# Hymba and PEER layer on one core: every fourth expert row of the first token half added on VectorE, and the steps around the gathers re-cut

## Chip, cores and metric

The kernel runs on one core of a Trainium2 chip. The metric is device time in microseconds of one execution. Before: 876.36 us, the median of three runs (872.04 to 880.57). What can be told from no change with such runs is about 1%.

## What is computed

The reference takes 256 tokens of width 1024 (float32) through one layer:

```python
h = rms_norm(x, attn_norm)
mq, mk, mv, dq, dk, dv = split(h @ w_in)          # six groups of 512 columns
a_out = moba_attention(rope(norm(mq)), rope(norm(mk)), mv)      # 8 heads x 64, causal
b_out = diff_attention(rope(norm(dq)), rope(norm(dk)), dv, lam) # 4 heads, softmax1 - lam*softmax2
x = x + concat(norm(a_out), norm(b_out)) @ w_out
# PEER, of xc = rms_norm(x):
q = (xc @ w_query).reshape(C, 8, 2, 128)
sc = einsum('thpd,hpnd->thpn', q, sub_keys)        # 8 heads x 2 x 128 scores
experts, gates = top 16 of the 16 x 16 sums of the two top 16's, softmax
u, vv = expert_down[experts], expert_up[experts]   # 128 rows of each per token
w = gates * gelu(einsum('cd,chkd->chk', xc, u))
x = x + einsum('chk,chkd->cd', w, vv)
```

With 256 positions there is one MoBA block, so group A is plain causal attention. Most of the data is the last part: 256 tokens x 128 experts x 8 KB of rows, 268 MB.

## The kernel before

The tokens form two halves of 128, A and B, with a token on each partition. The two expert tables lie side by side in DRAM, so that one indirect DMA (`in_uv_dram`, line 598) brings for one expert slot the down row and the up row of each of 128 tokens: 128 rows of 8 KB, 1.049 MB. There are 256 such **slots**, 0 to 127 for half A and 128 to 255 for half B. One slot is worked off so:

- `issue` (POOL, L598) starts the gather into a free buffer of a ring, if the slot's index is known (`ready`);
- `dot` (DVE, L608) multiplies the down row with the normalised token and sums: the slot's scalar `hdot`;
- `weigh` (ACT, L614, L615, L617) takes gelu, multiplies with the gate, and scales an identity matrix by the result: `dg`;
- `add` (PE, L627) multiplies `dg` with the up row, two products of 512 columns (each in float32 two passes, so x4 in the trace), summed in PSUM over the 128 slots of a half; then the buffer is free and `issue` is called.

`slots(1)` writes `dot` of slot n, `weigh` and, one slot behind, `add` of slot n-1. The buffers come in three pools: 4 (`gat0`) from the start, 5 more (`gat1`) once the projections of half B are through and their tiles freed, 6 more (`gat2`) once half B has left attention.

Ahead of the gathers run attention and output projection of half A, then `query`, `keys`, `route1` and `route2` for the first two PEER heads: product with the query weights, scores against the keys, the top 16 of each half by MAX8, FIND_INDEX8 and MATCH_REPLACE8 on DVE, candidate sums on POOL and DVE, index matching (`hit`, L550 on DVE and L553 on POOL) and the list `eid` of expert indices. This gives 32 ready slots. Up to there a scheduler orders the instructions. From `manual_schedule` on (end of the function) they stand as they are written: the generator `behind` yields all that is left of half A's routings and of half B (projections, attention, output projection, four routings) in small steps, and the main loop takes a fixed number of steps for each slot:

```python
while done[0] < NT * NSEL:
    slots(1)
    while steps < STEPS * (done[0] + 1):
        next(work, None)
        steps += 1
    issue()
```

Each engine works its queue strictly in order, so a step that waits holds up the slot work that is written behind it on the same engine. Weights come by DMAs from the SP queue (L88), 0.524 MB each, four for a group: `w_in` through a ring of eight tiles (`wts`), `peer_query` through four, `w_out` of half A through `wts` as well and of half B through four tiles that are there once attention is done (`wo2`).

Of the kernel before, what the change touches and what calls it, by code (L numbers as in the profile page):

```python
# [20 lines left out]
P = 128  # L21
# [27 lines left out]
STEPS = 1.45  # L49
# [3 lines left out]
def hymba_peer_kernel(ctx, tc, xT_d, x_d, an_d, fn_d, fnT_d, win_d, qkg_d, lam_d, og_d, wout_d,  # L53
# [9 lines left out]
    psA = ctx.enter_context(tc.tile_pool(name="psA", bufs=4, space=PSUM))  # L63
    psB = ctx.enter_context(tc.tile_pool(name="psB", bufs=2, space=PSUM))
# [3 lines left out]
    gat0 = ctx.enter_context(tc.tile_pool(name="gat0", bufs=RING0))  # L68
# [109 lines left out]
    def proj(ci, tt):  # L178
        p = pps[ci, tt] = psB.tile([P, 512], FT, name="psB")
        for k in range(KC):  # L180
            PE.matmul(p, lhsT=xT[tt][:, k], rhs=W[ci + 6 * tt][k // 2][:, k % 2], start=(k == 0), stop=(k == KC - 1))  # L181
            if k % 2:
                yield
# [215 lines left out]
    for g in (3, 0, 1):  # L399
        fetch(g, win_d[g], wts)  # L400
# [4 lines left out]
    for g in (5, 4):  # L405
        fetch(g, win_d[g], wts)
# [25 lines left out]
    for q in range(4):  # L432
        for n in range(2):
            fetch(("o", n, A), wout_d[n], wts, (q,))
# [31 lines left out]
    def query(tt, c4):  # L466
        w = W["q", c4]
        q = rt1.tile([P, 4, P], FT, name="qs", tag="qs")
        p = ps().rearrange("p (a b) -> p a b", b=P)
        for c in range(4):  # L470
            for k in range(KC):
                PE.matmul(p[:, c], lhsT=w[k // 2][:, k % 2, c * P:(c + 1) * P], rhs=xgT[tt][:, k],  # L472
                          start=(k == 0), stop=(k == KC - 1))
            if c < 3:
# [3 lines left out]
        yield

    def keys(tt, c4):  # L480
        sc = scp.tile([P, 4, NKEY], FT, name="sc")
        p = ps().rearrange("p (a b) -> p a b", b=NKEY)
        q = qs.pop((tt, c4))
        for c in range(4):
            PE.matmul(p[:, c], lhsT=q[:, c], rhs=sk[:, c4 * 4 + c], start=True, stop=True)  # L485
        S.activation(sc.rearrange("p a b -> p (a b)"), p.rearrange("p a b -> p (a b)"), AF.Copy, scale=r2[tt])  # L486
        scs[tt, c4] = sc
# [12 lines left out]
    def route1(tt, c4):  # L500
        sc = scs.pop((tt, c4))
        ts_ = rt1.tile([P, 2, 2, TOPK], FT, name="tops", tag="tops")
        ti = rt1.tile([P, 2, 2, TOPK], U32, name="topi", tag="topi")
        s2 = rt1.tile([P, 4, NKEY], FT, name="s2", tag="s2")
        hm = [(ts_[:, n // 2, n % 2], ti[:, n // 2, n % 2], sc[:, n], s2[:, n]) for n in range(4)]
# [24 lines left out]
        best = rt1.tile([P, 2, TOPK], FT, name="best", tag="best")  # L530
        pos = rt1.tile([P, 2, TOPK], U32, name="pos", tag="pos")
        s3 = rt1.tile([P, 2, NCAND], FT, name="s3", tag="s3")
        for h in range(2):
# [252 lines left out]
```

## Time and profile before

| | |
|---|---|
| runs | 876.36 us (872.04 to 880.57) |
| the profiled execution | 878.93 us, of which 877.2 us are the span from the first to the last instruction |
| granted TensorE clock, mean | 0.965 of full speed |
| busy in the span | PE 725.2, DVE 497.9, POOL 401.1, ACT 311.8 us |
| DMA | 323.16 MB, mean 368 GB/s; 268.85 MB of it by the gathers' queue |

Busy time of PE is modelled and long; the chain of waits and the tables of busy time by stretch say more. A DMA's time from issue to data is seen only in what waits for it.

### The profile page before, as it was taken

What the parts mean: (1) busy time and instruction counts of PE and PEld (TensorE: products, weight loads), DVE (VectorE), ACT (ScalarE), POOL (GpSimd) and SP (SyncE); (2) the same over time, 40 slices, a digit from 0 to 9 for tenths busy, and PEclk for the clock granted to TensorE, in tenths of its full rate; (3) what the DMA queues carried; (4) which work ended last, traced back from release to release, by engine and by line L of the source; (5) the groups of instructions that cost most, each with busy time, mean ns of one, the idle gap of its engine ahead of it and who ended that gap; (6) DMA issues with size and microseconds to landing.
All of it is one profiled execution on the core that took longest, in us unless ns stands there. A gap on an engine that the chain in (4) does not pass through costs nothing.

```text
span 877.2 us, 8338 instructions
## 1 busy us (share of the span) xinstructions
PE 725.2 (83%) x2156; PEld 337.4 (38%) x2156; DVE 497.9 (57%) x1364; ACT 311.8 (36%) x936; POOL 401.1 (46%) x426
## 2 busy tenths in 40 slices
PE   6998858597599888877989889799777787787776
PEld 2554543253245445433635545243222222222222
DVE  4753663764663776750577575874444454455443
ACT  1322112333242573621343352443333333333332
POOL 3310333562542573311654656675555555555540
PEclk9999969999999899988999999999999999999999
DMA  9969559989997999996999999999999999999993
GB/s 352 350 200 363 204 194 381 382 295 390 418 343 263 396 386 421 349 344 241 344 417 417 418 418 419 420 420 420 421 419 420 421 418 420 421 420 421 420 419 153
DMA packets 52687, 323.16 MB, mean 368 GB/s; under 512 B 6240, under 2 KB 6496, under 8 KB 19744
## 3 DMA queue, kind: packets, MB, share of 16 engines
q0 software_dynamic: 36944, 268.85, 76.0%
q1 hardware_dynamic: 15264, 53.12, 16.3%
q10 hardware_dynamic: 432, 0.66, 0.2%
q8 instruction: 18, 0.29, 0.1%
q14 instruction: 29, 0.24, 0.1%
HBM read 321.55 MB, written 1.05 MB: 368 GB/s over the span
## 4 chain that ended last, share of the span: by engine, by line
DMA 47%; PE 33%; DVE 9%; issue 5%; ACT 3%; POOL 2%; SPq 0%; DVEq 0%; POOLq 0%; ACTq 0%
DMA uv<-in_uv_dram,eid 43%; PE acc L627 14%; PE psB L181 7%; PE psA L472 4%; DVE uv L608 3%; DMA w<-in_wout_dram 3%; PE psB L350 3%; PE psA L252 1%; POOL hit L553 1%; PE psA L301 1%; POOL uv L598 1%; DMA w<-in_win_dram 1%; PE psA L485 1%; PE psA L251 1%; ACT dg L617 1%
## 5 line engine op out<-in xcount | busy, mean ns | idle before, releaser
L627 PE MATMUL acc<-uv,dg 128*128 128x512 f32 x1024 | 505.4, 625 | 110.3 <-ACT dg L617 107.6
L598 POOL DMA_INDIRECT uv<-in_uv_dram,eid x256 | 319.7, 1249 | 362.9 <-PE acc L627 182.6
L608 DVE SCALAR_TENSOR_TENSOR uv<-uv,xn 128x1024 f32<-128x1024 f32 x256 | 315.5, 1243 | 220.6 <-DMA uv<-in_uv_dram,eid 210.5
L627 PEld LDWEIGHTS acc<-uv,dg 128*128 128x128 f32 x1024 | 183.1, 194 | 395.5 <-ACT dg L617 235.5
L614 ACT ACTIVATE hdot<-hdot 128x1 f32<-128x1 f32 x256 | 51.3, 200 | 332.1 <-DVE uv L608 312.6
L617 ACT ACTIVATE dg<-ident,hdot 128x128 f32<-128x128 f32 x256 | 102.8, 402 | 48.5 <-PE acc L627 40.8
L181 PE MATMUL psB<-w,xT 128*128 128x512 f32 x192 | 90.8, 615 | 7.2 <-DMA w<-in_win_dram 7.2
L615 ACT ACTIVATE hdot<-hdot,gate 128x1 f32<-128x1 f32 x256 | 75.3, 294 | 8.3
L472 PEld LDWEIGHTS psA<-xgT,w 128*128 128x128 f32 x512 | 63.2, 198 | 11.7 <-issue 11.6
L472 PE MATMUL psA<-xgT,w 128*128 128x128 f32 x512 | 63.1, 280 | 0.0
L181 PEld LDWEIGHTS psB<-w,xT 128*128 128x128 f32 x192 | 36.5, 197 | 49.1 <-issue 46.6
L495 POOL TENSOR_TENSOR ci<-tf 128x4 f32<-128x4 f32 (+3 forms) x72 | 22.6, 344 | 56.8 <-DVE tf L523 56.7
L350 PE MATMUL psB<-w,mT 128*128 128x512 f32 x64 | 32.3, 640 | 8.3 <-DMA w<-in_wout_dram 7.6
L507 DVE MAX8 tops<-sc 128x8 f32<-128x128 f32 x32 | 7.0, 281 | 36.9 <-ACT sc L486 30.6
L567 DVE TENSOR_REDUCE ef<-hit 128x16 f32<-128x320 f32 (+1 forms) x16 | 11.5, 732 | 26.6 <-POOL hit L553 26.6
L553 POOL TENSOR_TENSOR hit<-hit,ci 128x160 f32<-128x160 f32 (+1 forms) x32 | 25.8, 838 | 0.9 <-DVE hit L550 0.7
L212 POOL TENSOR_TENSOR qt<-pr,rS 128x128 f32<-128x128 f32 (+1 forms) x24 | 14.1, 613 | 19.4 <-ACT pr L193 19.3
L358 DVE TENSOR_TENSOR x<-psB,x 128x512 f32<-128x512 f32 x4 | 2.8, 691 | 33.9 <-PE psB L350 33.9
L350 PEld LDWEIGHTS psB<-w,mT 128*128 128x128 f32 x64 | 12.4, 202 | 23.7 <-issue 12.8
L608 DVE DVE_READ_ACCUMULATOR uv<-uv,xn 128x1 f32 x256 | 21.4, 83 | 0.0
L476 ACT COPY qs<-psA 128x512 f32<-128x512 f32 x8 | 4.7, 582 | 33.2 <-PE psA L472 33.2
L226 PE MATMUL psA<-ident,qo 128*128 128x128 f32 x32 | 5.8, 311 | 12.4 <-DVE qo L219 12.4
(125 smaller groups left out, 410.3 us busy)
## 6 DMA issues: line engine op xcount, KB each, us to landing
w<-in_win_dram SPq DMA_DIRECT2D x48, 512.0 KB
w<-in_wq_dram SPq DMA_DIRECT2D x28, 512.0 KB
w<-in_wout_dram SPq DMA_DIRECT2D x16, 512.0 KB
uv<-in_uv_dram,eid POOLq DMA_INDIRECT x256
sk<-in_sk_dram SPq DMA_DIRECT2D x1, 1024.0 KB
out_dram<-x SPq DMA_DIRECT2D x4, 256.0 KB
xT<-in_xT_dram SPq DMA_DIRECT2D x2, 256.0 KB
x<-in_x_dram ACTq DMA_DIRECT2D x1, 512.0 KB
```

The source lines that it names most:

```text
L181: PE.matmul(p, lhsT=xT[tt][:, k], rhs=W[ci + 6 * tt][k // 2][:, k % 2], start=(k == 0), stop=(k == KC - 1))
L212: G.tensor_tensor(tv[:, :, m, a], prv[:, :, m, b], ropeS[tt][:, None, g0 + m, a].to_broadcast([P, nh, 32]), op=OP.mult)
L350: PE.matmul(wops[tt, n], lhsT=mixT[tt, MOBA if k < 4 else DIFF][:, k % 4], rhs=W["o", n, tt][k // 2][:, k % 2], start=(k == 0), stop=(k == ...
L472: PE.matmul(p[:, c], lhsT=w[k // 2][:, k % 2, c * P:(c + 1) * P], rhs=xgT[tt][:, k], start=(k == 0), stop=(k == KC - 1))
L495: eng.tensor_tensor(d, src[:, :, 1, b0:b0 + nb], src[:, :, 0, a0:a0 + 1].to_broadcast([P, 2, nb]), op=OP.add)
L553: G.tensor_tensor(e[:, h], e[:, h], ci[:, h, None, :n].to_broadcast([P, 8, n]), op=OP.mult)
L598: G.indirect_dma_start(out=rows[n], out_offset=None, in_=uv_d, in_offset=bass.IndirectOffsetOnAxis(ap=eid[tt][:, k:k + 1], axis=0))
L608: V.scalar_tensor_tensor(uv[:, :D], uv[:, :D], 1.0, xn[n // NSEL], op0=OP.mult, op1=OP.mult, accum_out=h)
L614: S.activation(h, h, AF.Gelu)
L615: S.activation(h, h, AF.Copy, scale=gate[n // NSEL][:, col:col + 1])
L617: S.activation(dg, ident, AF.Copy, scale=h)
L627: PE.matmul(acc[tt][:, c], lhsT=dg, rhs=uv[:, D + c * 512:D + (c + 1) * 512], start=(k == 0), stop=(k == NSEL - 1))
```

## The change

Five edits, which the diff shows together:

- **DVE adds.** For slots n of half A with n % 4 == 1 (32 slots) `weigh` stops after the gate, and `add` is one DVE instruction over 128x1024 that adds the up row times the slot's scalar to `x2[A]` in SBUF. The two products and `dg` are left out for these slots.
- **Finer steps.** A projection yields after each product of 512 columns (before: after two), a query after each four of 128, the output projection after each; STEPS goes from 1.45 to 2.0. One step is taken ahead of the first slot.
- **First routing by head.** The query of heads 0 and 1 is computed ahead, but scores and routing of head 0 alone; this gives 16 ready slots. Head 1 is the first work among the slots. The functions of the routing take the head and the number of heads.
- **Value weights kept.** Groups 5 and 4 (the values) of `w_in` stay in `wts` for half B, which projects 5, 4 and 2 ahead of the gathers (before: 2 and 3) and 3, 0, 1 among the slots (before: 0, 1, 5, 4). `w_out` of half A has eight tiles of its own, in room that `gat0` takes over.
- **Pools.** psA has 3 tiles for 4, psB 3 for 2, `hdot` 8 for 6.

```diff
-STEPS = 1.45
+STEPS = 2.0
+
+DVE_ADD = 4
...
-    psA = ctx.enter_context(tc.tile_pool(name="psA", bufs=4, space=PSUM))
-    psB = ctx.enter_context(tc.tile_pool(name="psB", bufs=2, space=PSUM))
+    psA = ctx.enter_context(tc.tile_pool(name="psA", bufs=3, space=PSUM))
+    psB = ctx.enter_context(tc.tile_pool(name="psB", bufs=3, space=PSUM))
...
-    gat0 = ctx.enter_context(tc.tile_pool(name="gat0", bufs=RING0))
+    wos = ExitStack()
+    wo1 = wos.enter_context(tc.tile_pool(name="wo1", bufs=8))
...
-            if k % 2:
-                yield
+            yield
...
-            fetch(("o", n, A), wout_d[n], wts, (q,))
+            fetch(("o", n, A), wout_d[n], wo1, (q,))
...
+    wos.close()
...
+        for a, b in parts:
+            p = ps().rearrange("p (a b) -> p a b", b=P)
+            for c in range(a, b):
+                for k in range(KC):
+                    PE.matmul(p[:, c], lhsT=w[k // 2][:, k % 2, c * P:(c + 1) * P], rhs=xgT[tt][:, k],
+                              start=(k == 0), stop=(k == KC - 1))
+                    if k % 4 == 3 and (c, k) != (b - 1, KC - 1):
+                        yield
+            S.copy(q[:, a:b], p[:, a:b])
+            yield
...
+    def choose(tt, c4, h0=0, nh=2):
+        yield from keys(tt, c4, 2 * h0, 2 * h0 + 2 * nh)
+        yield from route1(tt, c4, h0, nh)
+        yield
+        route2(tt, c4, h0, nh)
+        ready[0] += nh * TOPK
...
         S.activation(h, h, AF.Copy, scale=gate[n // NSEL][:, col:col + 1])
+        if n < NSEL and n % DVE_ADD == 1:
+            ready_w.append((n, h))
+            return
...
-        for c in range(2):
+        if n < NSEL and n % DVE_ADD == 1:
+            V.scalar_tensor_tensor(x2[tt], uv[:, D:], dg, x2[tt], op0=OP.mult, op1=OP.add)
+        for c in range(0 if n < NSEL and n % DVE_ADD == 1 else 2):
...
-    run(route(A, 0, 1))
+    run(query(A, 0, ((0, 2), (2, 4))))
+    load_q(1, wqp)
+    run(choose(A, 0, 0, 1))
...
-        fetch(g + 6, win_d[g], wts)
+        if g < 4:
+            fetch((g, B), win_d[g], wts)
+        else:
+            W[g, B] = W[g, A]
...
-    run(project(2), project(3))
+    run(project(5), project(4), project(2))
+    gat0 = ctx.enter_context(tc.tile_pool(name="gat0", bufs=RING0))
     rings += [gat0] * RING0
...
-        for g in (0, 1, 5, 4):
+        for g in (3, 0, 1):
             yield from project(g)
...
                     wout(B, n, k, psB)
-                yield
+                    yield
...
+        yield from choose(A, 0, 1, 1)
         yield from mix(route(A, 1, 2), f, 2, 1)
...
     work = behind()
+    for _ in range(1):
+        next(work)
```

POOL's queue before, around the first gathers; `ci` are candidate sums, `hit` index matches, `qt` and `qo` the rope of half B's projections, `uv<-in_uv_dram` a gather:

```order
L553 TENSOR_TENSOR hit_796<-hit_796,ci 128x160 x2
L553 TENSOR_TENSOR hit_800<-hit_800,ci 128x400 x2
L217 TENSOR_TENSOR qo<-qo,qt 128x512
L598 DMA uv<-in_uv_dram,eid_671 128x2048
L212 TENSOR_TENSOR qt<-pr,rS_833 128x8x32 x2
L598 DMA uv<-in_uv_dram,eid_671 128x2048
L217 TENSOR_TENSOR qo<-qo,qt 128x512
L598 DMA uv<-in_uv_dram,eid_671 128x2048 x11
```

The same place in POOL's queue after the change:

```order
L556 TENSOR_TENSOR hit_782<-hit_782,ci 128x160
L556 TENSOR_TENSOR hit_785<-hit_785,ci 128x400
L604 DMA uv<-in_uv_dram,eid_672 128x2048 x4
L214 TENSOR_TENSOR qt<-pr,rS_817 128x8x32 x2
L219 TENSOR_TENSOR qo<-qo,qt 128x512
L604 DMA uv<-in_uv_dram,eid_672 128x2048
L498 TENSOR_TENSOR ci<-tf 128x8
```

The matches ahead of the first gather are two instead of four, and four gathers stand ahead of the rope, which before stood between them.

DVE's queue before, from the first `dot` (`uv,hdot<-uv,xn`) on; `MAX`, `MAX_INDEX` and `MATCH_REPLACE` belong to the routing of heads 2 and 3:

```order
L608 SCALAR_TENSOR_TENSOR uv,hdot<-uv,xn_652 128x1024
L219 TENSOR_TENSOR qo<-qo,rsq 128x512
L608 SCALAR_TENSOR_TENSOR uv,hdot<-uv,xn_652 128x1024 x3
L507 MAX tops<-sc 128x8 x4
L608 SCALAR_TENSOR_TENSOR uv,hdot<-uv,xn_652 128x1024 x2
L510 MAX_INDEX topi<-tops,sc 128x8 x4
L513 MATCH_REPLACE s_1055<-tops,sc 128x128 x4
L608 SCALAR_TENSOR_TENSOR uv,hdot<-uv,xn_652 128x1024 x2
```

DVE's queue after the change at slots 5 to 12 (`x_105<-uv,hdot,x_105` is the new add; the first row is the `dot` of slots 5 and 6):

```order
L614 SCALAR_TENSOR_TENSOR uv,hdot<-uv,xn_653 128x1024 x2
L636 SCALAR_TENSOR_TENSOR x_105<-uv,hdot,x_105 128x1024
L614 SCALAR_TENSOR_TENSOR uv,hdot<-uv,xn_653 128x1024 x4
L636 SCALAR_TENSOR_TENSOR x_105<-uv,hdot,x_105 128x1024
L614 SCALAR_TENSOR_TENSOR uv,hdot<-uv,xn_653 128x1024
L510 MAX tops<-sc 128x8 x4
L614 SCALAR_TENSOR_TENSOR uv,hdot<-uv,xn_653 128x1024
```

An add of slot n stands behind the `dot` of slot n+1, so it also waits for that slot's rows. By the order of PE's queue, the scores of half B's attention begin at slot 44 before and at slot 54 after, and its residual stands at slot 80 to 82 in both.

## Rows read from the trace of the kernel before

**Rows 1.** Busy time of each engine by stretch, the span in seven parts
```profile
core 0: us, PE busy (x) PEld busy (x) DVE busy (x) ACT busy (x) POOL busy (x), PEclk, DMA share, GB/s
0.00:111.00 111.00, 97.63 (x348) 51.51 (x348) 62.91 (x237) 27.57 (x69) 26.94 (x45) 0.98 0.79 290
111.00:152.00 41.00, 30.21 (x123) 18.54 (x124) 18.95 (x56) 9.70 (x26) 13.46 (x13) 0.85 0.78 292
152.00:279.00 127.00, 101.50 (x326) 49.65 (x325) 74.71 (x220) 41.93 (x120) 60.02 (x77) 0.97 0.92 354
279.00:421.00 142.00, 120.13 (x370) 58.67 (x370) 80.21 (x210) 62.94 (x179) 53.72 (x60) 0.92 0.91 347
421.00:581.00 160.00, 141.13 (x514) 76.87 (x513) 117.97 (x410) 64.81 (x190) 100.38 (x125) 0.96 1.01 414
581.00:868.00 287.00, 230.65 (x473) 80.81 (x471) 140.65 (x228) 103.89 (x349) 146.59 (x108) 1.00 0.99 411
```

**Rows 2.** One source line in a stretch, L608: 152:279, 279:421, 421:581, 581:868
```profile
L608 DVE SCALAR_TENSOR_TENSOR uv<-uv,xn x36: 1210/1226/2679, 152.1 to 274.8; 128x1024 f32<-128x1024 f32 x36
L608 DVE SCALAR_TENSOR_TENSOR uv<-uv,xn x39: 1211/1222/3548, 279.2 to 417.5; 128x1024 f32<-128x1024 f32 x39
L608 DVE SCALAR_TENSOR_TENSOR uv<-uv,xn x59: 1206/1222/1324, 421.4 to 578.6; 128x1024 f32<-128x1024 f32 x59
L608 DVE SCALAR_TENSOR_TENSOR uv<-uv,xn x114: 1224/1226/1227, 581.1 to 865.8; 128x1024 f32<-128x1024 f32 x114
```

**Rows 3.** The chain that ended last, by line, 581:877, 279:421 and 152:279
```profile
by line: DMA uv<-in_uv_dram,eid 91.6%; issue 3.4%; PE acc L627 2.6%; DVE uv L608 0.4%; DVE x L634 0.2%; DVEq L782 0.2%; POOLq L598 0.2%; ACT dg L617 0.1%; ACT hdot L615 0.1%; POOLq L782 0.1%; ACT hdot L614 0.1%; DVEq L608 0.0%
by line: PE acc L627 40.8%; DMA w<-in_wout_dram 16.9%; PE psB L350 10.0%; PE psA L252 4.8%; PE psA L301 3.8%; issue 2.9%; PE psA L249 2.6%; ACT L614 1.8%; PE psA L251 1.8%; PE psA L289 1.5%; PE psB L181 1.2%; ACT ex L263 1.1%; ACT L558 0.9%
by line: DMA uv<-in_uv_dram,eid 42.6%; PE acc L627 17.0%; PE psB L181 9.5%; issue 8.9%; DVE uv L608 7.9%; PE psA L472 5.5%; POOL uv L598 3.1%; POOL hit L553 2.6%; ACT dg L617 1.0%; DVE cs L495 0.5%; ACT hdot L615 0.5%; ACT hdot L614 0.3%; D
```

**Rows 4.** Timeline of DVE and POOL, first routing to first gather
```profile
95.86 0.87 DVE L507 MAX8 tops<-sc 128x8 f32<-128x128 f32 x4 [5.59 <-ACT sc L486]
...
105.50 3.93 POOL L553 TENSOR_TENSOR hit<-hit,ci 128x160 f32<-128x160 f32 x4 [0.74 <-DVE hit L550]
109.39 1.26 POOL L217 TENSOR_TENSOR qo<-qo,qt 128x512 f32<-128x512 f32 x1
111.14 1.03 POOL L598 DMA_INDIRECT uv<-in_uv_dram,eid  x1 [0.49 <-DVE rs_a L123]
```

**Rows 5.** Timeline of DVE and POOL, first slots
```profile
118.66 1.22 DVE L608 SCALAR_TENSOR_TENSOR uv<-uv,xn 128x1024 f32<-128x1024 f32 x1
...
126.04 1.22 DVE L608 SCALAR_TENSOR_TENSOR uv<-uv,xn 128x1024 f32<-128x1024 f32 x1 [2.44 <-DMA uv<-in_uv_dram,eid]
...
129.91 0.94 POOL L598 DMA_INDIRECT uv<-in_uv_dram,eid  x1 [10.92 <-PE acc L627]
...
140.01 0.87 DVE L507 MAX8 tops<-sc 128x8 f32<-128x128 f32 x4 [12.73 <-ACT sc L486]
...
152.09 1.23 DVE L608 SCALAR_TENSOR_TENSOR uv<-uv,xn 128x1024 f32<-128x1024 f32 x1 [2.53 <-DMA uv<-in_uv_dram,eid]
```

**Rows 6.** Groups by line in 152:279: busy us, mean ns | idle before
```profile
L627 PE MATMUL acc<-uv,dg 128*128 128x512 f32 x138 | 69.5, 629 | 25.5 <-ACT dg L617 25.5
L608 DVE SCALAR_TENSOR_TENSOR uv<-uv,xn 128x1024 f32<-128x1024 f32 x36 | 46.4, 1288 | 49.3 <-DMA uv<-in_uv_dram,eid 44.2 <-ACT hdot L614 2.4 <-ACT qk L228 1.6
```

**Rows 7.** The chain in order of time, 279:425, pieces
```profile
305.61 9.87 PE acc L627 x16
...
369.51 15.34 DMA w<-in_wout_dram
384.89 4.12 PE psB L350 x6
389.01 2.14 PE acc L627 x4
391.15 1.72 PE psB L350 x4
392.87 1.72 PE acc L627 x4
394.58 0.87 PE psB L350 x2
...
395.47 8.71 DMA w<-in_wout_dram
```

**Rows 8.** One source line, L88 (loads of weights), from 111 us on
```profile
L88 SPq DMA_DIRECT2D w<-in_wq_dram x20: 328/368/547, 131.9 to 499.5; - x20
L88 SPq DMA_DIRECT2D w<-in_win_dram x12: 328/632/990, 133.9 to 211.8; - x12
L88 SPq DMA_DIRECT2D w<-in_wout_dram x8: 327/328/538, 368.7 to 396.3; - x8
```

**Rows 9.** Nearest row to the new add, and gather issues in 279:421 and 581:840
```profile
L376 DVE SCALAR_TENSOR_TENSOR xn<-x,r,fn x2: 1283/1284/1286, 88.7 to 426.4; 128x1024 f32<-128x1024 f32 x2
L598 POOL DMA_INDIRECT uv<-in_uv_dram,eid x44: 932/937/1966, 281.2 to 420.6; - x44
L598 POOL DMA_INDIRECT uv<-in_uv_dram,eid x104: 937/1371/1723, 581.0 to 838.1; - x104
```

More of the change, by code (lines that the diff above doesn't have):

```diff
@@ L399, in hymba_peer_kernel @@
     for g in (3, 0, 1):
[L400 removed]
+        fetch((g, A), win_d[g], wts)
     bcast(og, og_d, D)
@@ L464, in load_q, with query, keys @@
         fetch(("q", c4), wq_d[c4], pool)
-    def query(tt, c4):
+    def query(tt, c4, parts=((0, 4),)):
         w = W["q", c4]
         q = rt1.tile([P, 4, P], FT, name="qs", tag="qs")
[L469 to L474, printed above, removed]
-                yield
-        S.copy(q, p)
-        qs[tt, c4] = q
[L478 to L487, printed above, removed]
+        qs[tt, c4] = q
+        for a, b in parts:
[8 more added lines that the diff above has]
+            yield
+    def keys(tt, c4, a, b):
+        sc = scp.tile([P, 4, NKEY], FT, name="sc")[:, :b - a]
+        p = ps().rearrange("p (a b) -> p a b", b=NKEY)[:, :b - a]
+        for c in range(a, b):
+            PE.matmul(p[:, c - a], lhsT=qs[tt, c4][:, c], rhs=sk[:, c4 * 4 + c], start=True, stop=True)
+        S.activation(sc, p, AF.Copy, scale=r2[tt])
+        scs[tt, c4, a] = sc
         yield
@@ L529, in route1 @@
         yield
[L530 to L533, printed above, removed]
+        best = rt1.tile([P, 2, TOPK], FT, name="best", tag="best")[:, :nh]
+        pos = rt1.tile([P, 2, TOPK], U32, name="pos", tag="pos")[:, :nh]
+        s3 = rt1.tile([P, 2, NCAND], FT, name="s3", tag="s3")[:, :nh]
+        for h in range(nh):
             V.max(best[:, h, :8], cs[:, h])
-        for h in range(2):
+        for h in range(nh):
             V.max_index(pos[:, h, :8], best[:, h, :8], cs[:, h])
-        for h in range(2):
+        for h in range(nh):
             V.match_replace(s3[:, h], best[:, h, :8], cs[:, h], -3.0e38)
         yield
-        for h in range(2):
+        for h in range(nh):
             V.max(best[:, h, 8:], s3[:, h])
-        for h in range(2):
+        for h in range(nh):
             V.max_index(pos[:, h, 8:], best[:, h, 8:], s3[:, h])
-        posf = rt1.tile([P, 2, TOPK], FT, name="posf", tag="posf")
+        posf = rt1.tile([P, 2, TOPK], FT, name="posf", tag="posf")[:, :nh]
         V.tensor_copy(posf, pos)
@@ L713, in behind @@
         yield from mix(route(A, 3), f, 1, 1)
-        yield from f
+        for _ in f:
+            yield
         yield from route(B, 3, 2)
```

66 lines of the change are left out of this document (30 added, 36 removed).

## Prediction

> **What bounds the kernel now.** I read the busy table by stretch first, then the chain of waits, then single lines in the stretches where the chain changes its nature.
>
> From 421 us on the DMA engines move 411 to 414 GB/s [rows 1]. From 581 us the chain is 91.6% the gathers' own DMA [rows 3], and VectorE's `dot` comes at an even pace: 114 of them between 581.1 and 865.8, so 2.52 us a slot [rows 2]. Nothing that an engine does there can shorten the end; only fewer bytes or an earlier start of this steady stream can. Ahead of it the DMA moves 290, 292, 354 and 347 GB/s [rows 1]. Measured against 414 GB/s, the stretches from 111 to 421 us waste 41 x 0.29 + 127 x 0.14 + 142 x 0.16 = 53 us. That is what a change of the order can win.
>
> Who wastes it differs. Around 111 to 152 us the chain is broken up by queue order: the fifth gather waits 10.9 us for PE to free a buffer, and `dot` of slot 4 stands behind a MAX8 that waits 12.7 us for its scores [rows 5]. From 152 to 279 us, with four buffers, the chain is 42.6% gather, with PE pieces adding up to some 32% [rows 3]; VectorE waits 44.2 us for landings, and 36 slots take 127 us, 3.53 each [rows 2, 6]. From 279 to 421 us, attention and output projection of half B, the chain is PE's: 40.8% slot products, and 16.9% the wait for `w_out` [rows 3].
>
> So I forecast by landmarks: the first gather, slot 7, slot 54 (where attention begins after the change), slot 82, and the end. Before, these are: first issue 111.1, slot 7 at 152.1, slot 82 at 421.4 [rows 2, 4, 5]. From slot 82 both kernels have the same DMA work left, so the remaining 455.8 us are carried over.
>
> **The change part by part.**
>
> *First gather.* From the first MAX8 to the first issue 15.3 us pass [rows 4]. One head halves every round: five rounds over 128 columns like the one of 0.87 save at least 5 x 0.43 = 2.2; two instead of four matches on POOL save 3.93 / 2 = 2.0; half B's rope (1.26 on POOL) and its twin on DVE leave the queues ahead of the issue, together with halved match instructions some 2.3, an estimate from these rows. Sum 6.5 us: first issue at 104.6. Bounds: 4.2 (only the two sure items) to 8.
>
> *First slots.* The first gather's `dot` came 7.5 us after its issue [rows 4, 5]. DVE then has eight dots (1.31 with the read of the sum: 10.5), two adds (2.6), and routing and projection work, which before was 18.95 - 7 x 1.31 = 9.8 us in this stretch [rows 1, 2]; about as much, as half a routing and one projection stand there now. In sum 7.5 + 10.5 + 2.6 + 9.8 = 30.4; I add 2 us of waits: slot 7 at 137, 15 earlier than before. What allows it is that PE's first slot product now stands right behind the projections and the two turns are gone from in front of it. If half of the 12.7 us wait comes back, it is 143; the lower bound is 133.
>
> *Four-buffer stretch, slots 7 to 53.* 47 gathers at 2.52 are 118.4 us. Loads beside them: two query groups and two projection groups, 16 x 1.26 (half a gather's bytes each) = 20.2 us. The DMA floor is thus 138.6, or 2.95 a slot. PE's slot product falls from 69.5 / 36 = 1.93 a slot [rows 6] to three quarters, 1.45. DVE gets dearer: the nearest row to the add is a scale-and-multiply over 128x1024 with a scalar from SBUF, 1.28 us [rows 9]; `dot` itself took 1.23 and at worst 3.55 [rows 2]; I take 1.28, with 1.2 and 3.55 as ends. Before, DVE was busy 74.71 us in 36 slots, 2.08 each [rows 1]; other work than dots was 25.3. Now 47 x 1.31 + 12 x 1.28 + some 36 (one more routing) = 113, or 2.40 a slot. All three are below 3.53; the best is 2.95, and I take 3.2: 150 us, slot 54 at 287. Ends: 138.6 (DMA alone) and 47 x 3.53 = 166 (the pace of before).
>
> *Attention stretch, slots 54 to 81.* Before, 38 slots stood here, now 28, of which 21 have a PE product. The chain's slot products were 0.408 x 142 = 57.9 us; 21/38 of it is 32.0, a gain of 25.9. Seven adds of 1.28 are 9.0 on DVE; DVE is on this chain only in part, so I charge half, 4.5. PSUM pool psA with three tiles makes the second pair of score tiles wait for the first exponentials; no row shows it, between 0 and 8 us (two groups, about one `ex` and `mx` round each); I take 2. The waits for `w_out`, 15.3 and 8.7 us [rows 7], stay: its four tiles still come when attention ends. 142 - 25.9 + 6.5 = 122, slot 82 at 409. Ends: 110 (with fewer products PE also waits less for `dg`) and 142.
>
> *Value weights.* Eight loads, 4.2 MB, 10 us of DMA, are gone. But before the change 12 loads of `w_in` and 20 of the query weights follow the first gather [rows 8]; after it groups 3, 0 and 1 and the same queries do. The saved loads fall into the first 111 us, at 290 GB/s [rows 1], where PE and DVE set the pace: worth nothing. The same holds for the earlier `w_out` of half A.
>
> *Finer steps, STEPS 2.0.* They move work, cost no instruction, and their effect is in the slot numbers above.
>
> *Behind slot 82.* DVE has 117.97 of 160 us [rows 1]; eleven adds bring 14 more: 132. The DMA stays the limit.
>
> Sum: 137 + 150 + 122 = 409, against 421.4: 12 us less. The profiled execution took 878.93 us, so 866.9; it lies 0.3% above the median of the runs, and on their scale I predict 864 us.
>
> **The rivals.**
>
> *DMA alone sets the pace.* PE relieved, everything runs at the floor: 137 + 138.6 + 110 = 386, 36 less, 841 us. For it: between 581 and 868 us the stream needs no more than this. Against it: fifteen buffers there, four here.
>
> *Attention keeps its 142 us.* The steps come two to a slot, so that dependent steps (scores, maximum, exponential) meet without slot work between, and PE idles where it used to multiply. 137 + 150 + 142 = 429, 8 more: 884 us. For it: the chain hops to ACT and DVE in this stretch already. Against it: 40.8% of it is products of which many are gone.
>
> *The adds block POOL.* A gather's issue takes 0.937 us at the median in the attention stretch and 1.371 where dots run regularly beside it [rows 9]: one engine waits for the other. Fourteen adds fall into the time of four buffers, where each issue is urgent. At 0.43 each this is 6 us, at a whole add of 1.28 each 18: 137 + 150 + 122 + 18 = 427, 882 us. The Trainium skill (SBUF — State Buffer, section SBUF: two separate sides) says that a VectorE instruction with two SBUF inputs and a GpSimd instruction share a port pair that one of them holds for its whole length, the other being blocked. By that rule the add is such an instruction; the trace agrees for `dot`, with the two medians above.
>
> *Slower: VectorE becomes the bound with four buffers.* An add sits in order behind the next `dot`, so DVE's waits for landings cannot be filled. If they stay as long as before, 44.2 / 36 = 1.23 a slot [rows 6], and the 0.22 of other waits too, a slot takes 2.40 + 1.23 + 0.22 = 3.85, the stretch 181 us, and slot 82 comes at 440: 19 more, 895 us. It decides from 3.45 us a slot on; there the change only breaks even. Against it: waits for landings normally shrink when DVE comes later to them.
>
> **How the numbers follow.** A measurement of this kernel tells about 1% from no change. The forecast has 0.50, of which 0.44 lies over 1% below; DMA alone 0.14; attention unchanged 0.14 and the blocked POOL 0.08, both within 1%; VectorE-bound 0.14, of which 0.12 is over 1% slower. So faster 0.58, same 0.30, slower 0.12. The range goes from the DMA's case, 841, to just past the unchanged attention, 886; the likeliest case alone spans 850 to 876.
>
> **What would show it.** Right: first gather near 105 us, slot 7 near 137, the scores of half B's attention near 287, slot 82's `dot` near 409, an even 2.5 us from slot 141, and no wait for a matched index or a score above 5 us among the first slots. The slot products' share of the chain in attention should fall to about a quarter. Wrong: 3.5 us a slot or more with four buffers while DVE is over 85% busy (VectorE-bound); attention over 135 us with PE waiting for ACT or DVE; issues of 1.5 us and more beside the adds; or the DMA below 400 GB/s between slots 90 and 140, which would mean that the added DVE work limits there too.

## The result, and the profile after

885.6 us at the median of 11 runs (882.63 to 894.72), against 877.05 (872.04 to 881.01) for the kernel before in the same series: 1.0107 times as long, 95% interval 1.0074 to 1.0140. The forecast was 864 and faster, inside a range of 841 to 886; the change is slower by 1%. The profiled execution took 884.77 us, its span is 883.0 (before 877.2).

The landmarks are starts of `dot`, in us from the span's start. The forecast has slot 82 as its landmark; slot 84 stands here too, since the last step of half B's layer (projection, residual, norm) stands there in both kernels, and the last six buffers open.

| | before | forecast | after | after minus before, step by step |
|---|---|---|---|---|
| slot 0 | 118.7 | 112.1 | 112.8 | -5.9 |
| slot 7 | 152.1 | 137 | 138.4 | -7.8 |
| slot 54 | 313.2 | 287 | 309.8 | +10.3 |
| slot 82 | 421.4 | 409 | 422.8 | |
| slot 84 | 427.6 | | 432.7 | +8.5 (from slot 54) |
| slot 160 | 628.5 | | 635.4 | +1.7 |
| slot 255 | 868.3 | | 874.2 | -1.0 |

The steps sum to +5.8, the difference of the spans. So the change has a lead of 13.7 us at slot 7, is 5.1 us behind at slot 84, and hardly loses more after it. The table of busy time by stretch, cut at the same landmarks, answers to [rows 1]:

```profile
core 0: us, PE busy (x) PEld busy (x) DVE busy (x) ACT busy (x) POOL busy (x), PEclk, DMA share, GB/s
0.00:112.80 112.80, 104.97 (x364) 55.15 (x364) 56.25 (x208) 27.34 (x70) 25.86 (x45) 0.98 0.75 281
112.80:138.40 25.60, 14.37 (x51) 7.76 (x52) 21.70 (x75) 10.19 (x25) 14.69 (x22) 0.87 0.75 288
138.40:309.80 171.40, 123.96 (x395) 62.30 (x393) 115.98 (x321) 52.04 (x151) 75.46 (x93) 0.90 0.90 335
309.80:422.80 113.00, 83.03 (x268) 42.70 (x268) 68.45 (x161) 47.21 (x131) 42.95 (x48) 0.82 0.87 334
422.80:590.00 167.20, 127.73 (x473) 70.82 (x472) 137.09 (x424) 61.60 (x181) 106.70 (x125) 0.90 0.99 397
590.00:874.00 284.00, 230.49 (x476) 81.55 (x474) 140.16 (x228) 103.79 (x350) 146.01 (x108) 1.00 1.00 415
```

In the four-buffer stretch (third row) the DMA moves 335 GB/s where it moved 354 before, and VectorE is busy for 68%: on the mean neither is at its limit, yet a slot takes 3.65 us. The mean hides two states. The weights come in two bursts of eight loads, from 149 to 180 and from 210 to 242 us; cut there, the stretch reads:

```profile
149.40:180.30 30.90, 19.00 (x41) 7.51 (x40) 18.95 (x77) 8.23 (x26) 11.28 (x20) 0.89 1.01 405
180.30:209.80 29.50, 23.91 (x102) 14.60 (x103) 22.61 (x44) 11.52 (x31) 17.02 (x16) 0.94 0.84 299
209.80:242.10 32.30, 20.45 (x46) 8.52 (x45) 18.82 (x63) 8.31 (x26) 11.29 (x21) 0.92 1.01 412
242.10:309.80 67.70, 49.60 (x160) 25.06 (x158) 50.63 (x131) 21.11 (x61) 31.11 (x33) 0.86 0.82 286
```

Beside the loads the DMA is at its limit (405 and 412 GB/s). Outside of them it moves 299 and 286 GB/s, and no engine is full either: PE is busy for 81 and 73%, VectorE for 77 and 75%. There the time is lost. In the fifth row of the table by landmarks the DMA has 397 GB/s where before it ran at 414 from 421 us on.

The chain of waits of the four-buffer stretch, by line, answers to the last row of [rows 3]:

```profile
by line: DMA uv<-in_uv_dram,eid 34.5%; issue 22.1%; POOL uv L604 9.7%; DVE uv L614 8.3%; PE acc L638 7.0%; POOL hit L556 3.3%; POOL qt L214 2.8%; PE psB L184 1.5%; DVE x L636 1.4%; PE psA L477 1.0%; POOL qo L219 0.8%; ACT dg L626 0.7%; DVE 
```

The slot products went from 17.0% of the chain to 7.0%, and "issue", time in which the profile shows no wait, from 8.9% to 22.1%. But this can't be put down to the change, since the shares differ as much between two runs that do the same here. e3 and e12 below are one program up to slot 84 (e12's line numbers are one higher), with every product of this stretch on PE:

```profile
by line: DMA uv<-in_uv_dram,eid 34.0%; issue 23.8%; POOL uv L604 13.6%; DVE uv L614 8.2%; POOL hit L556 4.8%; PE acc L638 4.2%; POOL qt L214 2.6%; POOL qo L219 1.9%; ACT dg L626 0.7%; DVE s L516 0.6%; DVE topi L513 0.6%; DVE ef L570 0.6%; D
by line: DMA uv<-in_uv_dram,eid 38.2%; PE acc L639 19.6%; DVE uv L615 9.0%; PE psA L478 6.9%; PE psB L184 6.0%; issue 4.5%; DVE gate L561 2.4%; POOL hit L557 2.3%; POOL uv L605 1.0%; DVE hit L554 0.9%; ACT L621 0.8%; ACT dg L627 0.7%; DVE q
```

The same stretch's groups by line answer to [rows 6]:

```profile
L638 PE MATMUL acc<-uv,dg 128*128 128x512 f32 x144 | 80.1, 683 | 48.4 <-ACT dg L626 48.2
L614 DVE SCALAR_TENSOR_TENSOR uv<-uv,xn 128x1024 f32<-128x1024 f32 x47 | 59.9, 1274 | 50.2 <-DMA uv<-in_uv_dram,eid 49.5 <-issue 0.3 <-PE acc L638 0.3
L604 POOL DMA_INDIRECT uv<-in_uv_dram,eid x48 | 52.9, 1103 | 99.3 <-PE acc L638 54.4 <-DVE x L636 21.9 <-DVE s L516 5.8
L636 DVE SCALAR_TENSOR_TENSOR x<-uv,hdot,x 128x1024 f32<-128x1024 f32 x11 | 14.7, 1337 | 0.0
```

VectorE waits 49.5 us for landings although it got 14.7 us of adds, and POOL waits 21.9 us for adds to give their buffers back.

### The profile page after: what moved, and what is told of

It reads as the page before. It is cut to its first block, busy times and chain, and to the rows that moved or that the text cites. A ratio compares the mean times of both kernels' runs of the same rounds, so it can differ in the third digit from the quotient of the medians.

```text
span 883.0 us, 8001 instructions
## 1 busy us (share of the span) xinstructions
PE 688.5 (78%) x2028; PEld 321.6 (36%) x2028; DVE 542.2 (61%) x1417; ACT 303.1 (34%) x909; POOL 411.7 (47%) x438
## 4 chain that ended last, share of the span: by engine, by line
DMA 44%; PE 25%; DVE 14%; issue 8%; POOL 5%; ACT 3%; POOLq 0%; DVEq 0%; SPq 0%; ACTq 0%
DMA uv<-in_uv_dram,eid 41%; PE acc L638 8%; PE psB L184 6%; DVE uv L614 5%; PE psA L477 3%; PE psB L352 3%; POOL uv L604 3%; DVE x L636 1%; POOL hit L556 1%; DMA w<-in_win_dram 1%; DMA w<-in_wq_dram 1%; DMA w<-in_wout_dram 1%; PE psA L254 1%; PE psA L303 1%; ACT L620 1%
## 5 line engine op out<-in xcount | busy, mean ns | idle before, releaser
L638 PE MATMUL acc<-uv,dg 128*128 128x512 f32 x896 | 464.6, 649 | 151.2 <-ACT dg L626 149.8
L638 PEld LDWEIGHTS acc<-uv,dg 128*128 128x128 f32 x896 | 164.1, 200 | 407.8 <-ACT dg L626 269.4
L626 ACT ACTIVATE dg<-ident,hdot 128x128 f32<-128x128 f32 x224 | 89.9, 401 | 42.4 <-PE acc L638 35.8
L184 PE MATMUL psB<-w,xT 128*128 128x512 f32 x192 | 94.9, 631 | 7.2 <-DMA w<-in_win_dram 7.2
L477 PEld LDWEIGHTS psA<-xgT,w 128*128 128x128 f32 x512 | 65.0, 197 | 19.0 <-issue 18.7
L498 POOL TENSOR_TENSOR ci<-tf 128x4 f32<-128x4 f32 (+5 forms) x81 | 20.9, 291 | 58.8 <-DVE tf L526 58.8
L636 DVE SCALAR_TENSOR_TENSOR x<-uv,hdot,x 128x1024 f32<-128x1024 f32 x32 | 43.7, 1364 | 0.0
L556 POOL TENSOR_TENSOR hit<-hit,ci 128x160 f32<-128x160 f32 (+1 forms) x32 | 30.0, 968 | 0.5 <-DVE hit L553 0.4
L214 POOL TENSOR_TENSOR qt<-pr,rS 128x128 f32<-128x128 f32 (+1 forms) x24 | 18.2, 784 | 23.8 <-ACT pr L195 23.8
L570 DVE TENSOR_REDUCE ef<-hit 128x16 f32<-128x320 f32 (+3 forms) x18 | 11.8, 665 | 9.7 <-POOL hit L556 9.7
```

What stands on the lines that cost most here:

```text
L184: PE.matmul(p, lhsT=xT[tt][:, k], rhs=W[ci, tt][k // 2][:, k % 2], start=(k == 0), stop=(k == KC - 1))
L556: G.tensor_tensor(e[:, h], e[:, h], ci[:, h, None, :n].to_broadcast([P, 8, n]), op=OP.mult)
L626: S.activation(dg, ident, AF.Copy, scale=h)
L636: V.scalar_tensor_tensor(x2[tt], uv[:, D:], dg, x2[tt], op0=OP.mult, op1=OP.add)
L638: PE.matmul(acc[tt][:, c], lhsT=dg, rhs=uv[:, D + c * 512:D + (c + 1) * 512], start=(k == 0), stop=(k == NSEL - 1))
```

## The experiments

One table for all. "Pace" is us a slot from slot 7 to the slot at which half B's attention begins. "Attention part" runs from there to the slot at which the last step of half B's layer stands; how many slots it carries follows from the steps that are written between two slots. The ratio is to the kernel before in the same series.

| run | ratio, 95% interval | pace | attention part | slot 84 to 160 |
|---|---|---|---|---|
| before | | 3.52 | 40 slots, 145.5 us | 200.9 |
| after | 1.0107, 1.0074 to 1.0140 | 3.65 | 30, 122.9 | 202.6 |
| e1_no_adds | 1.0004, 0.9969 to 1.0039 | 3.49 | 30, 122.3 | 205.5 |
| e3_late_adds | 1.0000, 0.9967 to 1.0033 | 3.53 | 30, 122.6 | 203.4 |
| e5_add_first | 1.0047, 1.0012 to 1.0081 | 3.61 | 30, 126.8 | 202.5 |
| e2_adds_alone | 0.9955, 0.9921 to 0.9989 | 3.57 | 40, 140.9 | 199.8 |
| e7_ring5 | 0.9970, 0.9943 to 0.9997 | 3.45 | 30, 125.9 | 201.5 |
| e8_before_ring5 | 0.9848, 0.9806 to 0.9890 | 3.33 | 40, 140.3 | 200.1 |
| e10_six_weights | 1.0016, 0.9979 to 1.0052 | 3.53 | 40, 143.8 | 200.4 |
| e11_ring5_late_adds | 0.9849, 0.9805 to 0.9892 | 3.33 | 40, 142.0 | 199.1 |
| e6_slow_routes | 1.0051, 1.0018 to 1.0084 | 3.63 | 30, 127.1 | 197.8 |
| e12_late_adds_slow_routes | 0.9984, 0.9948 to 1.0020 | 3.56 | 30, 122.9 | 197.6 |
| e4_steps245 | 1.0167, 1.0119 to 1.0215 | 3.98 | 24, 113.0 | 191.5 |
| e9_coarse_steps | 0.9973, 0.9943 to 1.0004 | 3.74 | 34, 123.7 | 203.6 |
| e14_fine_before | 1.0027, 0.9991 to 1.0064 | 3.48 | 32, 125.5 | 200.8 |
| e16_steps17 | 1.0006, 0.9971 to 1.0041 | 3.55 | 36, 122.1 | 214.8 |
| e13_coarse_late_slow | 0.9915, 0.9881 to 0.9950 | 3.65 | 34, 124.6 | 199.9 |
| e17_coarse_late_145 | 0.9936, 0.9907 to 0.9966 | 3.54 | 38, 133.6 | 225.1 |
| e15_pools_before | 1.0140, 1.0096 to 1.0185 | 3.69 | 30, 122.6 | 201.2 |

One profile of a stretch is good to some 5 us: after and e6 are the same program up to slot 84, which came at 432.7 and 436.6, and so are e3 and e12, with 426.0 and 430.8. In e4, e16 and e17 attention does not end at slot 84 but at 68, 99 and 94, so their last column is not to be compared.

### The adds

e3 is the changed kernel with this in the three places that ask for an add slot; e1 has the condition false for all slots, and e2 puts the adds alone into the kernel before.

```diff
-        if n < NSEL and n % DVE_ADD == 1:
+        if 54 <= n < NSEL and n % DVE_ADD == 1:
```

> All edits of the change but the DVE adds: every slot is added by PE again. Theory A (the adds cost the time: each stands in DVE's queue behind the next dot and frees its buffer some 3 us later, and from slot 82 to 141 they fill DVE): slot 54 some 10 us earlier than 309.8, the stretch from slot 82 to 141 some 8 us shorter, the end near 868 to 872. Theory B (the finer steps and their rate cost it): 885 or more, as PE gets its product in every fourth slot back. Theory C (the pools and the kept value weights cost it): about 885 as well.

> The changed kernel with DVE adds only from slot 54 on (19 of 32); slots up to 53 are added by PE. Theory A, if the cost lies in the four-buffer stretch: slot 54 some 10 us earlier than 309.8 and the end near 875. Theory A, if it lies behind slot 82: slot 54 earlier, but slots 82 to 141 as long as in the changed kernel and the end 883 or later. Theory B: 885.

> The kernel before with the DVE adds alone (and eight hdot tiles, which they need). Theory A: 10 to 15 us slower than before, 887 to 891. Theory B or C: the adds relieve PE where it is waited for, 866 to 876.

Taking the adds out gives back the 1%; taking out only the 14 of the first 54 slots (18 are left, not 19) gives back as much. So the adds beside attention and the routings neither cost nor gain within what these runs tell, and those up to slot 53 cost about 1%. The groups of that stretch in e1:

```profile
L638 PE MATMUL acc<-uv,dg 128*128 128x512 f32 x188 | 93.5, 621 | 29.2 <-ACT dg L626 29.0
L614 DVE SCALAR_TENSOR_TENSOR uv<-uv,xn 128x1024 f32<-128x1024 f32 x47 | 59.5, 1266 | 56.2 <-DMA uv<-in_uv_dram,eid 45.1 <-PE acc L638 6.4 <-PE psA L477 4.5
L604 POOL DMA_INDIRECT uv<-in_uv_dram,eid x47 | 56.6, 1204 | 84.0 <-PE acc L638 58.1 <-DVE tops L519 5.3 <-DVE topi L522 5.2
```

The adds' 14.7 us on VectorE take 6 to 12 from the wait ahead of `dot`: it is 56.2 us in e1, 56.5 and 61.5 in e3 and e12, which have no adds in this stretch either, 50.2 after and 49.4 in e6. The rest lengthens the stretch, from 163.8, 166.1 and 167.2 us (e1, e3, e12) to 171.4 and 170.6 (after, e6). A buffer's round, from one `dot` in it to the next, is with four buffers the time of four slots: 14.2 us in e1 and 14.4 in e3, 14.9 after (means over slots 8 to 49). 0.5 to 0.6 us of the growth lies between the end of the issue and the next `dot` (7.5 and 7.6 to 8.1). Which wait makes it is not shown; differences this small are as large as those between two profiles of one program. The adds also leave gaps on PE: the granted clock of the stretch is 0.90 instead of 0.98, and 23% of the products less is only 14% less time (93.5 to 80.1 us), at 683 ns for 621. Against the clock as the cause stands e2, which has 0.87 in its four-buffer stretch and is not slower than the kernel before.

In the kernel before, the adds alone are 0.45% faster: its pace with four buffers hardly moves (3.52 to 3.57), and 40 slots beside attention take 140.9 us for 145.5, which is within what one profile tells. So by themselves the early adds cost little; the 1% is what they cost together with the other edits. e2 falls where theories B and C put it, not at theory A's 887 to 891; e1's 881.4, against 879.7 for the kernel before in that series, lies between theory A's 868 to 872 and the 885 of the others: the adds are not the whole loss.

e5 moves the add ahead of the next `dot`:

```diff
-            while len(ready_w) > (0 if last else 1):
+            early = lag[0] == 0 and ready_w[-1][0] % DVE_ADD == 1
+            while len(ready_w) > (0 if last or early else 1):
```

> The changed kernel; as long as there are four buffers, a DVE add is written right behind its own dot and weigh, ahead of the next dot. Theory L (with four buffers the round trip of a buffer sets the pace, and an add behind the next dot keeps its buffer some 3 us longer): slot 54 near 302 instead of 309.8, the end near 877. Rival P (the adds cost by the time they take on DVE and by holding up POOL): slot 54 at 310 or later, since DVE now also waits some 0.6 us for the gelu ahead of each add; 885 or more. Rival K (PE's lower granted clock in the gaps that the adds leave): slot 54 near 310, granted clock in the stretch as low as the 0.90 of the changed kernel.

The buffers of add slots do come free sooner, 3.1 us after `dot` instead of 5.2, but the next `dot` in them starts 9.2 us after the issue instead of 7.2: the round is 14.7 us, slot 54 at 308.0. So in the profile the earlier release brings nothing, since the `dot` in the buffer comes as much later: theory L's 302 did not come, nor rival P's 310 or later. But the timed run, 1.0047 for 1.0107, is 0.6% faster, with intervals that just overlap. How the cost of the early adds divides between their order and their time on VectorE is not shown.

### The buffers

The whole edit is e8's, on the kernel before. e7 has the rings on the changed kernel, and gets the room by leaving out the norm's gain and half of the sub-keys, so that it computes something else with the same instructions; e10 has the weight tiles alone; e11 is e8 with adds from slot 44 on.

```diff
-RING0 = 4
-RING1 = 5
+RING0 = 5
+RING1 = 4
-WRING = 8
+WRING = 6
```

> The changed kernel with five buffers at first and four more later. To make room for 8 KB a partition it leaves out the norm's gain vector in the rows that the dots multiply with, and half of the sub-keys (the first eight serve all sixteen), so other experts are chosen; the number of instructions and gathers is the same. Theory L: a round trip of 4 x 3.65 = 14.6 us over five buffers gives 2.9 a slot, at the DMA floor: slot 54 near 275 to 285, the end 862 to 872. Rival W (the work that stands between the slots in the queues of DVE and PE sets the pace): slot 54 at 303 or later, the end 880 or more.

> The kernel before with five buffers at first and four more later, paid for by six weight tiles instead of eight. Theory L: slot 7 to slot 44 in some 110 to 115 us instead of 131, the end 860 to 868, if the six weight tiles cost nothing ahead of the gathers (each us there comes on top). Rival W: slot 7 to 44 as before, 876 or more.

> The kernel before with six weight tiles instead of eight, and nothing else: the control to the run with five buffers. If the fifth buffer is what won there, 876 to 880. If fewer weight loads in flight won (less DMA beside the gathers), 864 to 868.

> The kernel before with five buffers first (six weight tiles) and DVE adds from slot 44 on, where attention begins: a version meant to beat both kernels. If the two gains add up (fifth buffer 1.5%, adds 0.45%), 859 to 862. If the fifth buffer already took from PE what the adds relieve, 864.

The fifth buffer does not give 2.9 us a slot: the round grows from 14.9 to 17.8 us with it. It is worth 0.2 us a slot in either kernel. In pace both theories miss: slot 54 came at 301.7, close to rival W's 303, and slots 7 to 44 took 123.0 us in e8, between L's 115 and the 130 of before. In time e8's 864.1 is where L had it, and e7's 874.4 is between the two. The two states of the stretch say why the gain is small. In e7, cut by its bursts of loads like the changed kernel above:

```profile
150.90:180.70 29.80, 19.18 (x42) 7.55 (x40) 18.02 (x78) 8.79 (x28) 12.81 (x21) 0.82 1.01 402
180.70:207.90 27.20, 23.88 (x98) 14.88 (x99) 22.53 (x44) 10.65 (x29) 19.69 (x16) 0.88 0.90 337
207.90:237.90 30.00, 21.01 (x49) 9.37 (x49) 16.89 (x54) 8.60 (x26) 12.38 (x21) 0.84 1.01 407
237.90:301.60 63.70, 47.81 (x155) 24.28 (x154) 51.18 (x139) 21.00 (x60) 31.05 (x33) 0.86 0.85 317
```

Beside the loads nothing is won, as the DMA is full in either kernel; outside of them it moves 337 and 317 GB/s where it moved 299 and 286. So there the number of buffers is a part of what holds the pace.

In the kernel before, the fifth buffer gains some 7 us from slot 7 to 44 and 3 to 5 beside attention (against before and e10), 1.5% in all. e10 says that it isn't the smaller weight ring. e8 and e11, 864.1 and 863.4 us, are the fastest of all runs and beat both kernels; adds on top of the fifth buffer bring nothing.

### The routings of half B

At the end of half B's layer the rate of steps, by which the main loop then counts, is lowered, in e6 to 1.2, in e12 (which has e3's adds) to 1.6:

```diff
         right.close()
+        rate[0] = 1.2
```

> The changed kernel, but from the end of half B's output projection on 1.2 steps a slot instead of 2.0, so that each routing of half B is spread over 17 slots instead of 10. Theory D (at 10 slots a routing VectorE needs 3.3 us a slot with its waits, more than the gathers and the query weights, and the fifteen buffers run full): no DMA dip between 540 and 590, the stretch from slot 84 to 141 shorter by 6 to 9 us, the end 876 to 879. Rival: the dip comes from the adds or from how late the stretch begins: no change, 884 or 885.

> The changed kernel with DVE adds only from slot 54 on and 1.6 steps a slot behind half B's output projection (12.5 slots a routing). If the two costs found are separate, the early adds 1.0% and the dense routings 0.5%: 0.5% below before, 871 to 873. If they are the same loss seen twice, 876.

The stretch from 540 to 590 us, of the changed kernel and of e6:

```profile
540.00:590.00 50.00, 37.92 (x93) 16.36 (x92) 43.18 (x119) 21.06 (x67) 32.60 (x36) 0.90 0.93 365
```

```profile
540.00:590.00 50.00, 40.29 (x137) 21.16 (x136) 36.89 (x113) 18.95 (x58) 29.28 (x34) 0.93 1.01 419
```

With the routings spread out the DMA dip is gone, and slots 84 to 160 take some 5 us less in both pairs (202.6 to 197.8, 203.4 to 197.6). e6's forecast of 6 to 9 us less from slot 84 to 141 did not come (160.6 us for 157.0): its routings reach to slot 151, so only 84 to 160 can be compared. In time it is 0.6% for e6, with intervals that just overlap, at 882.0 us instead of the 876 to 879 forecast, and 0.2% for e12 against e3, within the interval. e12's 877.4 is nearer to the 876 of one loss seen twice than to the 871 to 873 of two: that the early adds and the dense routings are separate costs is not shown. e1 shows the dip without adds (205.5 us, 340 GB/s from 540 to 583), and the kernel before, at 11 slots a routing instead of 10, has none (420 GB/s from 540 to 581). So the dip goes with the density of the routings and not with the adds.

### The steps

e4 is the changed kernel at STEPS 2.45, e16 at 1.7. e9 takes back the cut of the steps:

```diff
-STEPS = 2.0
+STEPS = 1.62
...
-            yield
+            if k % 2:
+                yield
...
-                    if k % 4 == 3 and (c, k) != (b - 1, KC - 1):
+                    if k == KC - 1 and c != b - 1:
...
-                    yield
+                yield
```

> The changed kernel with STEPS 2.45 for 2.0, so that attention of half B begins near slot 44, as before, and nine buffers are there ten slots earlier. Theory B in its form that the rate keeps the kernel on four buffers for too long: ten slots at 2.5 to 3 instead of 3.65 us, 5 to 10 us less, near 878. Theory A: more steps a slot lengthen each slot with four buffers, no gain, 883 to 890.

> The changed kernel with the steps cut as before (two products of a projection, a whole column block of a query, two products of the output projection to a step) and STEPS 1.62, at which half B's output projection ends at slot 84 as it did with 2.0. Theory S (the finer steps took PE off the chain, so that the adds have nothing left to relieve): the adds pay again as they do in the kernel before; slot 0 to 84 in some 305 us instead of 320, the end 868 to 874. Rival Q (the adds cost by their time on DVE whatever the cut of the steps): slot 0 to 84 in 315 us or more, the end 880 to 888.

> The kernel before with the finer steps alone, at STEPS 1.88, with which half B's output projection ends at slot 84 as before (attention begins at slot 52 instead of 44). If the finer steps cost by themselves: slot 0 to 84 some 8 us longer than 309, the end 882 to 888. If they cost only together with the adds: 876 to 880.

> The changed kernel with STEPS 1.7 for 2.0, the steps as finely cut as in it: attention of half B begins at slot 63 and its output projection ends at slot 99, so that 36 slots instead of 30 are carried in between, and a routing of half B takes 12 slots instead of 10. Theory V (the attention part has a length of its own, some 123 us, in which up to 34 to 36 slots ride free, and the rate of 2.0 carries too few): attention part 123 to 130 us, slot 99 some 8 us earlier than 479.1, the end 872 to 878. Rival F (the fine cut itself costs, whatever the rate): attention part some 36 x 4.1 = 148 us, the end 885 or more.

e4 is the slowest of all: attention begins at slot 44 as before, but each slot up to there takes 3.98 us, and theory B's 878 fell. With the fine cut and early adds the pace rises with the steps a slot: 3.55 us at 1.7 (e16), 3.65 at 2.0, 3.98 at 2.45, since a slot then has more of the projections, queries and loads beside it.

e9 pleads for theory S in time, but not in place: slots 0 to 84 took 310.0 us, between the 305 of S and the 315 of Q, its pace with four buffers is worse than after (3.74), and the gain is that 34 slots ride beside attention in 123.7 us. e16 then keeps the fine cut, lowers the rate alone, and carries 36 in 122.1. The attention parts of the changed kernel and of e16:

```profile
309.80:432.70 122.90, 92.93 (x317) 49.14 (x317) 76.19 (x179) 50.09 (x139) 47.59 (x53) 0.83 0.87 335
```

```profile
337.30:459.40 122.10, 96.97 (x311) 48.58 (x309) 82.73 (x194) 54.86 (x155) 55.88 (x58) 0.87 0.94 372
```

Same length, six more slots, 372 GB/s instead of 335. The attention part has a length of its own, 122 to 127 us for 30 to 36 slots; 24 slots take 113.0, and only from 38 on does it grow (133.6, at 40 slots 140 to 146). At 2.0 steps a slot it carries too few, and the six or ten that it leaves behind are worked off ahead of it with four buffers. The fine cut itself costs little (e14: 1.0027, its interval holds 1); the rate that came with it costs 1% (e16 against after). A part of this 1% may be the routings of half B, which e16 also spreads, over 12 slots each; e9 leaves them at 10 and gains 1.3%.

> The changed kernel with all three suspected costs undone: steps cut as before at STEPS 1.62, DVE adds only from slot 54 on, 1.3 steps a slot behind half B's output projection. If the three are separate (1.3%, 1.0% and 0.5% of the changed kernel), 860 to 866, with slot 0 to 84 in some 300 us and 84 to 160 in 198. If they are shares of one loss, no better than the best of them alone: 872 to 876.

> The changed kernel with the steps cut as before, adds from slot 54 on and 1.3 steps a slot behind the output projection, as in the run with all three costs undone, but STEPS 1.45 instead of 1.62: attention from slot 56 to 94, 38 slots instead of 34. Theory V: 38 slots are past what rides free, attention part 130 to 138 us, and the end within 4 us of that run, 866 to 872. If a lower rate always wins: 862 or less.

> The changed kernel with four tiles in psA and two in psB, as before. If psA's third tile less is what lengthens the way from slot 54 to slot 84 (in the changed kernel 123 us): 5 us or more less there, the end 877 to 880. If not: within 2 us of the changed kernel, 883 to 887.

e13, with rate, early adds and dense routings undone, is 1.9% below the changed kernel, between what separate losses (some 3%) and one loss (1.3%) would give: the three costs overlap. Against before its profile is 9.8 us shorter, and 6.1 of that are the earlier first `dot` alone. e17 came as theory V has it, 133.6 us for 38 slots and 870.6 in all. e15 clears the PSUM pools: 122.6 us for 122.9.

## Why the prediction was wrong

That 885.6 lies inside the range at all is luck: the upper end, 886, stood for an attention stretch of 142 us, and that stretch took 113.

*First gather, first slots: right.* 103.7 for 104.6, slot 7 at 138.4 for 137.

*Four-buffer stretch, "I take 3.2: 150 us": the step that failed.* It took 171.4 us, 3.65 a slot, above the upper end of 166; 21 us too long, more than the 18 by which the whole span missed (883.0 for 864.8). The sum took the highest floor of a single engine, 2.95 of the DMA, and went less than half of the way from there to the 3.53 of before. (PE's floor of 1.45 counted the slot products alone; with the steps' products PE is busy for 123.96 us, 2.64 a slot. VectorE has 2.47 for 2.40.) Only beside the two bursts of loads did a floor hold: there the DMA was full. In the 97 us between and behind them it moved 299 and 286 GB/s, and no engine was full. The runs show three things that move the pace there: the early adds (3.49, 3.53 and 3.56 without them in e1, e3 and e12, 3.65 and 3.63 with them after and in e6, so 4 to 8 us of the 21), the steps a slot (3.55 to 3.98), and a fifth buffer (3.45). So the relief of PE, which was to bring the 3.2, bought nothing here: without it the stretch takes 164 to 167 us, the upper end of the forecast, and with it 171. How the way from the floor up to those 164 to 167 us divides over buffers, steps and queue order stays open. The rival of the DMA alone, with 138.6 us, had the limit for the bursts and not for the rest.

*The slower rival, VectorE as the bound.* It had the right place. Its point of decision (3.45) was passed, but e1 passes it too, without adds. VectorE was busy for 68%, not over 85%, and the pace is 3.65, not 3.85: waits for landings did shrink when VectorE came later, as I held against it, but by 6 to 12 us of the 14.7 and not by all.

*Attention stretch, 122 us: 113.0, better than forecast, for a wrong reason.* I took the chain's 40.8% of slot products as what the slots cost there and credited 25.9 us for the 17 products less. The share did fall to about a quarter, as forecast (24.4% from slot 54 to 84), but the credit is not in the products: e1 has 30 of them in this part and after 23, and both take 122 to 123 us, and e16 carries more slots in the same time. The length is attention's own; moving slots out of it saves time from 40 down to 36 and next to nothing below, and each moved slot then costs time with four buffers. The rival that attention keeps its 142 us had a length that does not follow the products, with the wrong number; that dependent steps which slots no longer cover set it is argued and not shown.

*Behind slot 82, "455.8 carried over": 460.2.* 3.7 us between slots 82 and 84 (9.9 for 6.2), and the routings, at ten slots each, go with a DMA below 400 GB/s (365 from 540 to 590 us), as the last sentence on what would show it wrong had it, though with the rate and not the adds.

*The adds block POOL: the wait is real, its price is not.* A gather's issue that starts while an add runs does wait for the add's end, as the last section shows. But few meet one: in this stretch a single issue started under an add, 0.04 us behind its start, and that one was not held:

```profile
270.49 1.29 DVE L636 SCALAR_TENSOR_TENSOR x<-uv,hdot,x 128x1024 f32<-128x1024 f32 x1
270.53 0.94 POOL L604 DMA_INDIRECT uv<-in_uv_dram,eid  x1 [2.53 <-PE acc L638]
272.05 0.94 POOL L604 DMA_INDIRECT uv<-in_uv_dram,eid  x1 [0.59 <-DVE x L636]
```

The third row's issue is the one that stands behind the add in the program and waits for it anyway. So the mean issue of the stretch is 1103 and 1160 ns with adds (after, e6) and 1204, 1176 and 1095 without (e1, e3, e12): the rival's 6 to 18 us are not there. Issues of 1.5 us and more under an add, its sign, occur four times, all behind slot 54.

*Value weights, worth nothing: not tried alone.*

## What to carry to other kernels

Where few buffers are in flight, the busy sums of single engines are floors that need not be near, and work added to an engine with idle time can lengthen a slot all the same. A buffer's round divided by the buffers is no price either: a fifth buffer gave 3.45 where that rule says 2.9. Cut such a stretch where its loads begin and end before a limit is read from a mean. A serial part that other work rides beside can have a length of its own: find how many slots it carries free before moving any out of it. When steps are cut finer, the rate has to be found anew, part by part.

## What the runs showed of the hardware

POOL's work can hold up a tiny VectorE instruction for its whole length. The subtraction of the gates over 128x32 (L560) takes 185 and 197 ns when it does not run beside `hit` on POOL, 596 to 601 in four cases beside it, in which it ends 0.06 us behind the first of two, and once 4.08 us, until the last of five POOL instructions in a row was through, at 256.05 (in e6, the same program there, 4.08 us as well):

```profile
252.01 4.08 DVE L560 TENSOR_TENSOR gate<-best 128x32 f32<-128x32 f32 x1
252.06 1.27 POOL L219 TENSOR_TENSOR qo<-qo,qt 128x512 f32<-128x512 f32 x1
253.28 2.77 POOL L556 TENSOR_TENSOR hit<-hit,ci 128x160 f32<-128x160 f32 x4
256.02 1.21 DVE L614 SCALAR_TENSOR_TENSOR uv<-uv,xn 128x1024 f32<-128x1024 f32 x1
```

The other way round, `dot` and add hold up a gather's issue:

```profile
313.76 1.28 DVE L636 SCALAR_TENSOR_TENSOR x<-uv,hdot,x 128x1024 f32<-128x1024 f32 x1
314.06 1.81 POOL L604 DMA_INDIRECT uv<-in_uv_dram,eid  x1 [0.15 <-POOL ci L500]
```

An issue takes 0.94 us by itself. One that starts well inside a `dot` or an add ends 0.80 to 0.85 us after the end of that instruction, over all runs: 55 issues did so under adds, 2825 under dots. That is also why the issue's median beside regular dots is 1.37 us. The Trainium skill (SBUF — State Buffer, section SBUF: two separate sides) has an exclusive lock between a VectorE instruction with two SBUF inputs and a GpSimd instruction that reads SBUF: the one that starts first has the shared ports for its whole length. These traces agree, for the issue of an indirect DMA too; the 4.08 us differ from it in that one wait there lasted over five instructions.

A long gap on PE was paid for once more behind it. After 7.45 us without work the four products of a slot took 3.78 us, at a granted clock of 0.50 (258.7 to 262.5 us); 6 us later they took 1.88, at 1.00 (264.9 to 266.8):

```profile
258.69 3.78 PE L638 MATMUL acc<-uv,dg 128*128 128x512 f32 x4 [7.45 <-ACT dg L626]
...
264.90 1.88 PE L638 MATMUL acc<-uv,dg 128*128 128x512 f32 x4
```

Those are the two levels of the clock, 1.2 and 2.4 GHz.
